# The row of 1/rms of the first feed-forward stage is turned inside the tail gate chunk

## The chip, the cores and the metric

The kernel runs on one core of a Trainium2 chip. The metric is device time in microseconds (us), the median of several runs. Besides these runs one execution was recorded by the hardware profiler; every time that is read from a trace below belongs to that one execution. PE is TensorE (its weight loads are listed apart as PEld), DVE is VectorE, ACT is ScalarE, POOL is GpSimd, and SP issues most of the DMAs.

## What is computed

One layer of an encoder: a half-step feed-forward stage (FFN), a mixing stage of Fourier and attention heads, a second FFN, and a last norm, on 512 tokens of width 1024, all in float32. The change lies in the opening of the first FFN:

```python
def rms_norm(x, g):
    xf = x.astype(jnp.float32)
    y = xf * lax.rsqrt(jnp.mean(xf * xf, axis=-1, keepdims=True) + EPS)
    return (y * g.astype(jnp.float32)).astype(x.dtype)

def swiglu(h, w_gate, w_up, w_down):
    return (jax.nn.silu(h @ w_gate) * (h @ w_up)) @ w_down

x = x + 0.5 * swiglu(rms_norm(x, ffn1_norm), ffn1_w_gate, ffn1_w_up, ffn1_w_down)
```

## The kernel before

The activations lie transposed, features on partitions and tokens along the free dimension, as 8 tiles of 128x512 (`x[k]`). A float32 product is made of three passes of a fast format: every operand is split into a high part (a cast on ACT) and a low part (the rest, a subtraction on DVE: `lows`, L130, or, for some weights, a negation on ACT, L159, with a DMA from POOL that adds the original, L160), and high x high, high x low and low x high are summed in one PSUM bank.

The factor 1/rms of a token multiplies a whole row of the product, so it is put off: PE multiplies the gained but not yet normalised `x`, and the factor comes in when a bank is read. For that the factor has to lie along the free dimension, the same on all partitions. `Norm.sum` (L244) adds the squares with PE, `mean` (L251, DVE) and `power` (L258, POOL) give `r`, one factor per token in a column of 128x4, and `row` (L263, L271) turns it: four transposes on PE write the bank `rp`, and ACT copies that bank to `rb` in SBUF.

What reads `rp` and `rb` is the rest of the opening:

- `evacuate` (L659 to L674) reads the gate and up banks of one chunk pair with `rb` (DVE), takes the silu (ACT), multiplies (DVE) and splits the product into its high and low parts `at` (L663 ACT, L130 DVE). This also frees the banks for later chunks.
- `operands` (L349 to L356 and L359) makes, for i = 0 to 3, the tile `b_i` from `x`, the gains and `rp`, then the differences `t_i`, and splits them into the parts `rt`. These are what the later groups of the stage multiply, by a Strassen-like scheme of seven products (`seven`). The tile `b_i` lies in a pool of two buffers, which it shares with `raw_g`, the gate weights of that scheme; so the load of the first `raw_g` waits until everything that reads `b_2` is done.

PE and SP follow the order in which the program is written. On ACT and DVE that holds for the first half of the opening; after it the order of their instructions is worked out when the program is built, by a scheduler that has its own costs. Every engine then runs its instructions in that order.

PE's order in the opening is: the products of chunks 0 to 3 over k = 0 to 7 (L769, twelve matmuls for each k), the tail chunk 42 (`gate(2 * NF)`, 24 matmuls, the 64 last gate and 64 last up columns), the chunks 4 to 7 (24 matmuls each), and then the down projections dn_0 to dn_7 of this group of chunks (11 matmuls each). The weights of dn_d are loaded by SP (`raw_dn`), cast by ACT (L172) and given their low part by DVE (L130); the third matmul of dn_d is the first to read that low part. SP's queue has, after `raw_dn` 0 to 2, the first `raw_g` and `raw_u`, and behind them `raw_dn` 3 to 7.

The row is turned at (k, n) = (7, 4), that is, after the first four of the twelve matmuls of k = 7. The second FFN gives its own place for it (`gate(1, {3: row})`).

Of the kernel before, what the change touches and what calls it, by code (L numbers as in the profile page):

```python
# [18 lines left out]
NF = F // P  # L19
# [69 lines left out]
def encoder(ctx, tc, A, out):  # L89
# [19 lines left out]
    def bank(name):  # L109
        return pp.tile([P, S], F32, tag="bank", name=name)  # L110
# [68 lines left out]
    def turned(ap):  # L179
        return ap.rearrange("p (a b c) -> p b a c", b=4, c=4)  # L180
# [12 lines left out]
    class Norm:  # L193
# [71 lines left out]
        def row(self, c0=0, c1=4):  # L265

            ps = bank(f"rp{self.n}_{c0}")
            for c in range(c0, c1):
                self.turn(ps, c)
            t = slice(c0 * P, c1 * P)  # L270
            nc.scalar.copy(self.rb[:, t], ps[:, t])  # L271
            return ps
# [11 lines left out]
    def ffn(norm, after, wgu, wd, wdt, groups, opening, closing):  # L284
# [6 lines left out]
        with tc.tile_pool(name=f"act{n_}", bufs=1) as ap, tc.tile_pool(name=f"sums{n_}", bufs=2) as sp:  # L291
# [7 lines left out]
            def place(j):  # L299
                where[j] = free.pop(0)  # L300
                return where[j]
# [8 lines left out]
            def gate(c, between={}, by_dma=False):  # L310
                whi, wlo = weights(wgu[c], f"gu{n_}_{c}", by_dma=by_dma)
                ps = bank(f"gu{n_}_{c}")
                for k in range(KD):
                    between.get(k, int)()
                    product(ps, whi[:, k, :], wlo[:, k, :], hh[k], hl[k], k == 0, k == KD - 1, turn=True)
                return ps
# [48 lines left out]
            def back(ts):  # L365
                plain[:] = [t for t in plain if all(t is not q for q in ts)]
# [213 lines left out]
            for gi, group in enumerate(groups):  # L580
                last = gi == len(groups) - 1
                ahead = []
                if gi:
                    rest = seven(range(group[0] + 1, min(group[-1] + 2, NF)), ready)
                else:
                    lent = [acts[:, FRONT + i * KD * P : FRONT + (i + 1) * KD * P] for i in range(PLACES - 4, PLACES)]
                    plain.extend(lent)
                    row = []
                    pss = dict(enumerate(opening(gate, lambda: norm.column([norm.acc]), lambda: row.append(norm.row()))))
                    back(lent[:2])  # L590
                    due, parts, left = [*pss, "t"], list(range(KH)), range(2 * len(pss), 2 * n_plain)
                    pss["t"] = [gate(2 * NF)]
                    tail_weights()
                    for i, c in enumerate(left):
                        pss.setdefault(c // 2, []).append(gate(c, by_dma=i in (1,) if n_ else i > 0))
                        if due:
                            j = due.pop(0)
                            evacuate(at[:, place(j)], n_, pss[j], norm)
                        if c % 2 and c != left[-1]:
                            due.append(c // 2)  # L600
                        while len(parts) * len(left) > (len(left) - 1 - i) * KH:
                            o = parts.pop(0)
                            operands(row[0], o, o + 1)

                    def rest():
                        evacuate(at[:, place(n_plain - 1)], n_, pss[n_plain - 1], norm)
# [114 lines left out]
    def opening1(gate, column, row):  # L721

        pss = [bank(f"gu0_{c}") for c in range(4)]
        ws = []
        ts = slice(0, HALF), slice(HALF, S)
        cs = slice(0, 2), slice(2, 4)

        def highs(i, k):
            n0.scale_high(k)
            hi, _ = ws[i]  # L730
            nc.scalar.copy(hi[:, k % 2], raws[i][:, k % 2])

        def first_operands():

            hi, lo = ws[0]
            for t, c in zip(ts, cs):
                n0.scale_high(0, nc.vector, t)
                n0.scale_low(0, t)
                nc.scalar.copy(hi[:, 0, c], raws[0][:, 0, c])
            for c in cs:  # L740
                lows(lo[:, 0, c], raws[0][:, 0, c], hi[:, 0, c])

        def first_products():

            hi, lo = ws[0]
            for t, c0, m in [(ts[0], c, m) for c in cs for m in (hh, hl)] + [(ts[1], c, m) for m in (hh, hl) for c in cs]:
                for c in range(c0.start, c0.stop):
                    nc.tensor.matmul(
                        turned(pss[c][:, t]), hi[:, 0, c], turned(m[0][:, t]), start=m is hh and t is ts[0], stop=False,
                        skip_group_check=True,  # L750
                    )
            for c in range(4):
                nc.tensor.matmul(
                    turned(pss[c]), lo[:, 0, c], turned(hh[0]), start=False, stop=False, skip_group_check=True
                )

        def weight_lows(i, k):
            hi, lo = ws[i]
            lows(lo[:, k % 2], raws[i][:, k % 2], hi[:, k % 2])

        def products(k):
            hi, lo = ws[k // 2]
            passes = [(c, w, m) for w, m in ((hi, hh), (hi, hl), (lo, hh)) for c in range(4)]
            for n, (c, w, m) in enumerate(passes):
                if (k, n) == (6, 8):
                    sums()
                if (k, n) == (7, 4):
                    row()
                nc.tensor.matmul(  # L769
                    turned(pss[c]), w[:, k % 2, c], turned(m[k]), start=False, stop=k == KD - 1 and w is lo,  # L770
                    skip_group_check=True,
                )

        ss = []

        def sums():
            ss.append(bank("ss0"))
            for c in range(4):
                n0.sum(ss[0], c, [n0.acc])

        with tc.manual_schedule(engines={mybir.EngineType.Activation, mybir.EngineType.DVE}):
            for k in range(KD):
                i = k // 2
                if k % 2 == 0:
                    ws.append(tuple(slot().rearrange("p (a c b) -> p a c b", a=2, b=P) for _ in range(2)))
                if k == 0:
                    first_operands()
                    continue
                highs(i, k)
                if k < KD - 1:  # L790
                    n0.scale_low(k)
                    weight_lows(i, k)
                for j in {3: range(0, 4), 5: (4, 5), 6: (6, 7)}.get(k, ()):
                    n0.sums(j)
            first_products()
            for k in range(1, KD - 1):
                products(k)
            n0.scale_low(KD - 1)
            n0.mean(ss[0], 0, 4)
            n0.power(0, 4)  # L800
            weight_lows(KH - 1, KD - 1)
            products(KD - 1)
        nc.sync.dma_start(out=qkg, in_=A["qkg"])
        nc.sync.dma_start(out=fb, in_=A["fb"])
        return [pss[0:2], pss[2:4]]
# [795 lines left out]
```

## Time and profile before

| what | value |
|---|---|
| median of 3 runs | 818.72 us |
| lowest and highest run | 818.27 and 1692.98 us |
| time of the profiled execution | 818.38 us |
| its span, first to last instruction | 816.6 us |
| busy: PE, DVE, ACT, POOL | 99%, 80%, 62%, 8% of the span |
| granted TensorE clock, mean | 0.998 |

The median and the profiled execution agree within 0.34 us; one of the three runs took twice as long. Between span and time of the profiled execution lie 1.8 us. In a row of the timeline stand the start and the duration in us, the engine, the line, the operation, what it writes and reads, its shape, how many instructions are merged in the row, and in brackets the idle time of the engine before it with what ended it. Rows of one engine overlap a little: the next instruction starts some 0.08 us before the end of the last on DVE, some 0.1 us on ACT, and a matmul every 0.22 us though one is listed with 0.38 us.

### The profile page before, as it was taken

How to read it: one execution, taken by the hardware profiler on the slowest of the kernel's cores; microseconds unless marked ns; L12 is line 12 of the kernel's file. 1: busy time of each engine (PE TensorE's matmuls, PEld its weight loads, DVE VectorE, ACT ScalarE, POOL GpSimd, SP SyncE). 2: the span in 40 equal slices, each digit the busy share in tenths (PEclk: the TensorE clock that was granted, in tenths of full speed). 3: DMA queues.
4: the chain of work that ended last, by engine and by line, in shares of the span. 5: the costliest groups of instructions: out<-in, count | busy, mean ns of one | idle time of the engine just before them, and what ended most of it. 6: DMA issues, size and time to landing. Idle time of an engine off the chain costs nothing.

```text
span 816.6 us, 13031 instructions
## 1 busy us (share of the span) xinstructions
PE 809.8 (99%) x4943; PEld 729.3 (89%) x4943; DVE 652.4 (80%) x1083; ACT 503.2 (62%) x871; POOL 67.7 (8%) x75
## 2 busy tenths in 40 slices
PE   9999999999999999999999999999999999999997
PEld 7888998899989998889998888889988998899987
DVE  7997997489856857799998578999955997489674
ACT  7873774267624735699998449557733674267462
POOL 0320000000000000221000003100100000000001
PEclk9999999999999999999999999999999999999999
DMA  7874553345443423442201236554543553345222
GB/s 258 198 172 172 146 132 89 125 130 168 85 151 89 126 67 117 130 149 65 65 26 53 78 109 140 128 188 143 133 116 110 154 145 81 132 130 143 62 78 103
DMA packets 37823, 99.75 MB, mean 122 GB/s; under 512 B 4481, under 2 KB 11265, under 8 KB 37761
## 3 DMA queue, kind: packets, MB, share of 16 engines
q1 hardware_dynamic: 28064, 82.87, 31.2%
q0 software_dynamic: 8832, 15.34, 11.1%
q8 instruction: 38, 0.62, 0.3%
q10 hardware_dynamic: 864, 0.72, 0.3%
q14 instruction: 25, 0.20, 0.1%
HBM read 93.41 MB, written 2.10 MB: 117 GB/s over the span
## 4 chain that ended last, share of the span: by engine, by line
PE 94%; DMA 2%; ACT 1%; DVE 1%; issue 1%; POOL 0%; SPq 0%; POOLq 0%; DVEq 0%; ACTq 0%
PE dn L186 26%; PE r L436 11%; PE mix L186 8%; PE gu L186 8%; PE r L441 8%; PE q L436 4%; PE r L432 4%; PE q L441 4%; PE p L432 4%; PE q L432 4%; PE p L441 2%; PE mix L1267 2%; PE mix L1233 2%; PE mix L1071 1%; PE mix L1072 1%; PE mix L1073 1%
## 5 line engine op out<-in xcount | busy, mean ns | idle before, releaser
L186 PE MATMUL dn<-at,ring 128*128 128x512 f32 x900 | 202.7, 380 | 0.0
L186 PEld LDWEIGHTS dn<-at,ring 128*128 128x128 f32 x900 | 168.0, 188 | 28.9 <-DVE ring L130 0.3
L441 PE MATMUL r<-rt,ring 128*128 128x256 f32 x560 | 154.3, 276 | 0.0
L436 PE MATMUL r<-rt,ring 128*128 128x256 f32 x840 | 147.0, 276 | 0.0
L436 PEld LDWEIGHTS r<-rt,ring 128*128 128x128 f32 x840 | 127.0, 188 | 1.6
L441 PEld LDWEIGHTS r<-rt,ring 128*128 128x128 f32 x560 | 105.1, 188 | 0.2
L391 ACT CAST ring<-s 128x1024 fp32r<-128x1024 f32 x70 | 73.6, 1051 | 35.4 <-PE r L436 16.4
L130 DVE TENSOR_TENSOR ring<-s,ring 128x1024 fp32r<-128x1024 f32 x70 | 85.1, 1216 | 12.6 <-ACT ring L391 10.3
L575 DVE SCALAR_TENSOR_TENSOR gx<-dn,gx 128x512 f32<-128x512 f32 x61 | 41.8, 688 | 63.0 <-PE dn L186 63.0
L172 ACT CAST ring<-raw_dn 128x768 fp32r<-128x768 f32 (+3 forms) x58 | 45.3, 784 | 71.3 <-PE dn L186 55.2
L441 PE MATMUL q<-rt,ring 128*128 128x256 f32 x280 | 77.0, 275 | 0.0
L160 POOL DMA_DIRECT2D ring<-in_wgu x38 | 32.9, 866 | 470.1 <-ACT u L450 372.0
L130 DVE TENSOR_TENSOR ring<-raw_dn,ring 128x768 fp32r<-128x768 f32 (+3 forms) x58 | 51.5, 890 | 9.9 <-ACT ring L172 5.9
L441 PEld LDWEIGHTS q<-rt,ring 128*128 128x128 f32 x280 | 52.6, 188 | 0.0
L130 DVE TENSOR_TENSOR ring<-raw_g,ring 128x1024 fp32r<-128x1024 f32 x35 | 42.6, 1218 | 10.1 <-PE p L432 9.5
L436 PE MATMUL q<-rt,ring 128*128 128x256 f32 x280 | 49.8, 277 | 0.0
L432 PE MATMUL r<-rt,ring 128*128 128x512 f32 x140 | 48.7, 384 | 0.2 <-ACT u L489 0.2
L186 PE MATMUL gu<-ring 128*128 128x512 f32 x216 | 48.9, 381 | 0.0
L432 PE MATMUL q<-rt,ring 128*128 128x512 f32 x140 | 48.3, 382 | 0.0
L432 PE MATMUL p<-rt,ring 128*128 128x512 f32 x140 | 48.3, 382 | 0.0
L186 PEld LDWEIGHTS gu<-ring 128*128 128x128 f32 x216 | 40.4, 188 | 6.9
L391 ACT CAST ring<-raw_g 128x1024 fp32r<-128x1024 f32 x35 | 36.8, 1051 | 15.0 <-DMA raw_g<-in_wgu 12.0
(282 smaller groups left out, 1659.3 us busy)
## 6 DMA issues: line engine op xcount, KB each, us to landing
raw_g<-in_wgu SPq DMA_DIRECT2D x35, 512.0 KB, 3.7
raw_u<-in_wgu SPq DMA_DIRECT2D x35, 512.0 KB, 4.4
raw_dn<-in_wd SPq DMA_DIRECT2D x40, 384.0 KB, 3.2
ring<-in_wgu POOLq DMA_DIRECT2D x35, 256.0 KB, 4.3
raw_gu<-in_wgu SPq DMA_DIRECT2D x12, 512.0 KB, 3.6
raw_o<-in_wo SPq DMA_DIRECT2D x8, 512.0 KB, 3.5
raw_dn<-in_wd SPq DMA_DIRECT2D x8, 448.0 KB, 3.4
raw_wq<-in_wins SPq DMA_DIRECT2D x4, 512.0 KB, 3.6
```

The source lines that it names most:

```text
L130: nc.vector.tensor_tensor(out=lo, in0=src, in1=asf(hi), op=ALU.subtract)
L160: nc.gpsimd.dma_start(out=lo, in_=src, accum_op=ALU.add)
L172: nc.scalar.copy(hi[:, :n, :], raw[:, :n, :])
L186: nc.tensor.matmul(ps, a, b, start=first and b is mhi and a is whi, stop=last and a is wlo)
L391: nc.scalar.copy(hi, src)
L432: nc.tensor.matmul(turned(ps), whi[:, ks], turned(m), start=start, stop=False, skip_group_check=True)
L436: nc.tensor.matmul(ps[:, t], whi[:, ks], m[:, o * HALF :][:, t], start=start and o == 0, stop=False, skip_group_check=True,)
L441: nc.tensor.matmul(o, wlo[:, ks], m, start=False, stop=stop, skip_group_check=True)
L575: nc.vector.scalar_tensor_tensor(out=x[d][:, t], in0=ps[:, t], scalar=0.5, in1=x[d][:, t], op0=ALU.mult, op1=ALU.add)
L1071: nc.tensor.matmul(ps, hh[k][:, cs], whi[:, a, :], start=k == 0, stop=False)
L1233: nc.tensor.transpose(pts[n][:, c * P : (c + 1) * P], prob[t, b, c][:, kc * P : (kc + 1) * P], ident)
L1267: nc.tensor.matmul(turned(outs[t, b]), w, turned(p), start=kc == 0 and i == 0, stop=kc == 3 and i == 1)
```

## The change

The row is no longer turned within the products of chunks 0 to 3, but one chunk later, within the tail chunk, before its products of k = 1, that is, after its first three matmuls. The second FFN, whose opening has filled `row` by then, is built as before.

```diff
-                    pss["t"] = [gate(2 * NF)]
+                    pss["t"] = [gate(2 * NF, {} if row else {1: lambda: row.append(norm.row())})]
...
                 if (k, n) == (6, 8):
                     sums()
-                if (k, n) == (7, 4):
-                    row()
                 nc.tensor.matmul(
```

On PE and SP nothing else moves, and on POOL one DMA of the opening goes ahead of two others; lines behind the removed ones have a number lower by two. ACT and DVE get another order in the whole opening. In the rows below, `gu_c` is the bank and `raw_gu_c` the raw weights of chunk c, `g0p` and `u0p` are the gate and up tiles of an evacuation, `s_0_4` are sums of weights of the first `raw_g` and `raw_u`, and `dn_d` is the bank of a down projection.

ACT, around the copy of the row (L271), before:

```order
L172 CAST ring<-raw_gu_4_354 128x1024
L271 COPY rb_102<-rp_0_298 128x512
L172 CAST at_129<-raw_gu_5_408 128x1024
L359 CAST rt_130<-b_0_391 128x256
L159 ACTIVATE at_129<-at_129 128x1024
L359 CAST rt_130<-b_0_391 128x2x256
```

ACT, the same place, now:

```order
L172 CAST ring<-raw_gu_4_354 128x1024
L172 CAST at_129<-raw_gu_5_408 128x1024
L159 ACTIVATE at_129<-at_129 128x1024
L271 COPY rb_102<-rp_0_317 128x512
L661 ACTIVATE g0p<-g0p 128x512
L359 CAST rt_130<-b_0_391 128x256
```

The copy of the row now stands behind the cast and the negation of the weights of chunk 5.

DVE, from the last subtraction that reads `b_2` (its third row `t_2_506`) to the low part of the weights of dn_2, before:

```order
L356 TENSOR_TENSOR t_2_506<-b_2_503,t_2_506 128x256
L130 TENSOR_TENSOR rt_130<-t_2_506,rt_130 128x3x256
L356 TENSOR_TENSOR t_3_562<-b_3_559,t_3_562 128x256
L130 TENSOR_TENSOR at_129<-u0p,at_129 64x512
L659 TENSOR_TENSOR g0p<-gu_6_469,rb_102 128x512
L130 TENSOR_TENSOR rt_130<-t_3_562,rt_130 128x3x256
L130 TENSOR_TENSOR at_129<-u0p,at_129 128x512
L130 TENSOR_TENSOR rt_130<-t_2_506,rt_130 128x256
L130 TENSOR_TENSOR rt_130<-t_3_562,rt_130 128x256
L130 TENSOR_TENSOR ring<-raw_dn_2_0_620,ring 128x384
```

DVE, up to that same subtraction, which is the last row here, now:

```order
L356 TENSOR_TENSOR t_3_562<-b_3_559 128x256 x2
L130 TENSOR_TENSOR at_129<-u0p,at_129 64x512
L662 TENSOR_TENSOR u0p<-g0p,u0p 128x512
L659 TENSOR_TENSOR g0p<-gu_6_469,rb_102 128x512
L356 TENSOR_TENSOR t_2_506<-b_2_503,t_2_506 128x256
L356 TENSOR_TENSOR t_3_562<-b_3_559,t_3_562 128x256
L130 TENSOR_TENSOR ring<-raw_dn_2_0_620,ring 128x384
L130 TENSOR_TENSOR at_129<-u0p,at_129 128x512
L356 TENSOR_TENSOR t_2_506<-b_2_503,t_2_506 128x256
```

Four instructions that stood behind that subtraction stand ahead of it now: the low parts of `u0p` (64x512 and 128x512), the reading of bank gu_6, and the low part of the weights of dn_2.

DVE, from the low part of the first `raw_g` on, with the low part of the weights of dn_3 (`raw_dn_3`), before:

```order
L130 TENSOR_TENSOR ring<-raw_g_4_635,ring 128x1024
L406 TENSOR_TENSOR s_0_4_639<-raw_u_4_636 128x512
L406 TENSOR_TENSOR s_0_4_640<-raw_g_4_635,raw_u_4_636 128x512
L660 TENSOR_TENSOR u0p<-gu_7_526,rb_102 128x512
L406 TENSOR_TENSOR s_0_4_639<-s_0_4_639,raw_g_4_635 128x512
L575 SCALAR_TENSOR_TENSOR gx<-dn_0_0_577,gx 128x512
L130 TENSOR_TENSOR at_129<-raw_dn_3_0_645,at_129 128x384
L662 TENSOR_TENSOR u0p<-g0p,u0p 128x512
L406 TENSOR_TENSOR s_0_4_640<-raw_g_4_635,s_0_4_639 128x512
L575 SCALAR_TENSOR_TENSOR gx<-dn_1_0_602,gx 128x512
```

DVE, the same place, now:

```order
L660 TENSOR_TENSOR u0p<-gu_7_526,rb_102 128x512
L130 TENSOR_TENSOR rt_130<-t_3_562,rt_130 128x3x256
L130 TENSOR_TENSOR rt_130<-t_2_506,rt_130 128x256
L130 TENSOR_TENSOR rt_130<-t_3_562,rt_130 128x256
L662 TENSOR_TENSOR u0p<-g0p,u0p 128x512
L575 SCALAR_TENSOR_TENSOR gx<-dn_0_0_577,gx 128x512
L130 TENSOR_TENSOR ring<-raw_g_4_635,ring 128x1024
L406 TENSOR_TENSOR s_0_4_639<-raw_u_4_636 128x512
L406 TENSOR_TENSOR s_0_4_640<-raw_g_4_635,raw_u_4_636 128x512
L575 SCALAR_TENSOR_TENSOR gx<-dn_1_0_602,gx 128x512
L130 TENSOR_TENSOR at_129<-u0p,at_129 128x512
L130 TENSOR_TENSOR at_129<-raw_dn_3_0_645,at_129 128x384
```

Ahead of the low part of `raw_dn_3` now stand L662, L575 of dn_1 and one more low part of `u0p`, which stood behind it; one L406 that stood ahead of it stands behind it.

## The prediction

> **What bounds the kernel now.** I read the page first, then PE's waits over the whole run, then the timeline of the opening engine by engine. The first fence is the page's row of busy times, then PE's waits (us in total, times, longest).
>
> ```profile
> PE 809.8 (99%) x4943; PEld 729.3 (89%) x4943; DVE 652.4 (80%) x1083; ACT 503.2 (62%) x871; POOL 67.7 (8%) x75
> ...
> PE busy L702 <- PEq L1584: 0.8, 1, 0.8
> PE rp L263 <- POOL r L258: 0.6, 1, 0.6
> PE r L432 <- ACT u L489: 0.2, 1, 0.2
> ```
>
> PE is the bound nearly everywhere, so a change counts by what it does to PE's few waits. The second wait, 0.6 us, is the row being turned before POOL has made `r`. The timeline shows it:
>
> ```profile
> 22.88 2.04 PE L769 MATMUL gu<-ring,at 128*128 128x512 f32 x8
> 23.94 1.53 POOL L258 TENSOR_TENSOR r<-ms,mhalf 128x4 f32<-128x4 f32 x1 [22.63 <-DVE ms L251]
> 25.52 0.65 PE L263 MATMUL rp<-ident,r 128*128 128x128 f32 x4 [0.60 <-POOL r L258]
> 25.93 2.01 PE L769 MATMUL gu<-ring,at 128*128 128x512 f32 x8
> 27.78 10.72 PE L186 MATMUL gu<-ring 128*128 128x512 f32 x48
> ```
>
> One matmul is issued every (10.72 - 0.38)/47 = 0.22 us. The last one ahead of the transposes starts at 22.88 + 2.04 - 0.38 = 24.54, so the next could start at 24.76; the transposes start at 25.52. The loss is 0.76 us of issue time, a little more than the listed 0.60.
>
> The second thing to see is DVE. The windows view gives, for the stretch from DVE's first use of the row to its first later idle time, length, then busy time and count of PE, PEld, DVE, ACT and POOL, PEclk, DMA share and GB/s:
>
> ```profile
> 26.83:54.45 27.62, 27.62 (x128) 23.55 (x127) 27.50 (x52) 24.94 (x44) 10.13 (x10) 1.00 0.91 203
> ```
>
> DVE works 27.50 of 27.62 us: its queue is full for 28 us, and it begins when the row is there. PE is not held only because everything it takes from that queue comes just early enough.
>
> **The change part by part.** *PE's wait goes.* `r` is ready at 23.94 + 1.53 = 25.47. After the change eight matmuls (1.76) and three of the tail chunk (0.66) go from 24.76 on, so PE comes to the transposes at 27.18, 1.7 us after `r`. The four transposes are the same four; their price moves with them. Gain: 0.76 us. The cover is good, since the 1.7 us do not hang on any other transfer.
>
> *The row comes later to ACT.* `rp` is complete at 27.18 + 0.65 = 27.83 instead of 26.17. But by the new order its copy (L271) stands behind the cast and the negation of the weights of chunk 5. These are their rows, the copy's, and the load of those weights with its time to landing:
>
> ```profile
> 26.21 0.59 ACT L271 COPY rb<-rp 128x512 f32<-128x512 f32 x1 [1.42 <-PE rp L263]
> 27.36 1.05 ACT L172 CAST at<-raw_gu 128x1024 fp32r<-128x1024 f32 x1 [0.56 <-PE gu L769]
> 28.62 1.06 ACT L159 ACTIVATE at<-at 128x1024 fp32r<-128x1024 f32 x1
> 29.58 0.60 ACT L359 CAST rt<-b 128x512 fp32r<-128x512 f32 x1
> ...
> 23.74 0.33 SPq L154 DMA_DIRECT2D raw_gu<-in_wgu  x1
> ...
> DMA to landing us min/median/max: 3.5/3.5/3.5
> ```
>
> The cast needs its weights, which land at 23.74 + 3.5 = 27.24, hardly before the matmul that the page names as its releaser. That matmul will be over sooner, the landing will not: the cast starts at about 27.3. The negation reads what the cast writes and starts at 27.3 + 1.05 = 28.35; the next instruction follows 0.96 later (28.62 to 29.58 above), so the copy starts at 29.3 and ends at 29.9. Who waits behind it: all of DVE's new order starts with L659, which reads `rb`.
>
> *DVE starts later.* Its rows that carry the rest:
>
> ```profile
> 26.83 2.72 DVE L349 SCALAR_TENSOR_TENSOR b<-gx,rp 128x512 f32<-128x512 f32 x4 [0.79 <-ACT rb L271]
> ...
> 48.78 0.42 DVE L356 TENSOR_TENSOR t<-b,t 128x256 f32<-128x256 f32 x1
> ...
> 50.43 0.69 DVE L130 TENSOR_TENSOR at<-u0p,at 64x512 fp32r<-64x512 f32 x1
> 51.16 0.69 DVE L659 TENSOR_TENSOR g0p<-gu,rb 128x512 f32<-128x512 f32 x1
> ...
> 52.63 0.68 DVE L130 TENSOR_TENSOR at<-u0p,at 128x512 fp32r<-128x512 f32 x1
> ...
> 53.90 0.55 DVE L130 TENSOR_TENSOR ring<-raw_dn,ring 128x384 fp32r<-128x384 f32 x1
> 54.81 1.22 DVE L130 TENSOR_TENSOR ring<-raw_g,ring 128x1024 fp32r<-128x1024 f32 x1 [0.35 <-ACT ring L391]
> 55.95 0.68 DVE L406 TENSOR_TENSOR s<-raw_u 128x512 f32<-128x512 f32 x1
> ...
> 58.95 0.55 DVE L130 TENSOR_TENSOR at<-raw_dn,at 128x384 fp32r<-128x384 f32 x1
> ```
>
> Start 29.95 instead of 26.83: 3.1 us late. A full queue can't make that up; it can only be reordered. The place where PE feels it is dn_3, whose low weights are the last row above (end 59.50). PE's row:
>
> ```profile
> 61.44 0.82 PE L186 MATMUL dn<-at 128*128 128x512 f32 x3
> ```
>
> The third of these matmuls, at 61.44 + 0.44 = 61.88, is the first that reads them: they are 2.4 us early. After the change: 59.50 + 3.1 for the later start; plus three instructions that now stand ahead (L662, L575 of dn_1, a low part of `u0p`) less one that now stands behind (L406), each about 0.60 to the next start, so + 1.2; less DVE's idle time before 54.81, which is filled (0.35 + 0.08 of overlap). That is 63.4.
>
> *A second way to the same place.* SP's first `raw_g` waits for the readers of `b_2`, and `raw_dn` 3 is queued behind it. SP's waits and the load's rows:
>
> ```profile
> SPq L383 <- DMA rt<-b: 10.4, 2, 7.9
> ...
> 50.27 0.33 SPq L383 DMA_DIRECT2D raw_g<-in_wgu  x1
> ...
> DMA to landing us min/median/max: 3.4/3.4/3.4
> ```
>
> Before, a DMA that reads `b_2` ended that wait; DVE's last subtraction had ended at 48.78 + 0.42 = 49.20. After, that subtraction ends 3.1 later and behind four more instructions (0.61 + 0.60 + 0.60 + 0.47 = 2.3, from the rows at 50.43 to 53.90, less the overlap): 54.6. The load is issued then and lands at 58.0; ACT's cast takes 1.05 (as the one of chunk 5, the same shape), so DVE can take the low part of `raw_g` at 59.1. It gets there by its own queue at about 59.2. The two ends fall together, so DVE does not idle and neither alone would save much. From 59.15: 1.14 to the next start, four instructions of 0.60, then 0.55: 63.2 to 63.3. I take 63.3.
>
> *The sum.* Without a new wait PE would want that low part at 61.88 - 0.76 = 61.12. It gets it at 63.3: a new wait of 2.2 us. Net + 1.45 us, or, simpler, the third matmul of dn_3 starts at 63.3 instead of 61.88, and the gain is lost within the wait. Behind it PE goes on at its old pace: the low part of dn_4 follows in DVE's queue directly, 0.47 later, and each dn takes PE 11 x 0.22 = 2.4 us. From the group behind, the orders are the same again. So 818.38 + 1.4 = 819.8 us. The profiled run stands 0.34 under the median of the runs shown, which I take into the range.
>
> Bounds: the term that no row shows is how the reordered DVE queue meets ACT's. Were DVE never kept waiting by ACT, 63.3 stands; were every one of the three instructions moved ahead of `raw_dn` 3 to find its input late by its own 0.60, it is 65.1, net + 3.2. From below, if the cast of chunk 5 did not hold up the copy (27.9 instead of 29.3), the wait shrinks by 1.4 to 0.8 and the net is nothing. I take the middle value since all its steps are rows.
>
> One moved DMA needs a price, that of POOL for chunk 6, which goes ahead of two of `b_1`. The negation ahead of it, the DMA with its landing, and PE's chunk 6:
>
> ```profile
> 34.17 1.06 ACT L159 ACTIVATE ring<-ring 128x1024 fp32r<-128x1024 f32 x1
> ...
> 35.53 0.91 POOL L160 DMA_DIRECT2D ring<-in_wgu  x1 [0.98 <-ACT ring L159]
> ...
> DMA to landing us min/median/max: 6.3/6.3/6.3
> 43.62 1.70 PE L186 MATMUL gu<-ring 128*128 128x512 f32 x7
> ```
>
> It landed at 41.9; the third matmul of chunk 6 (44.06) wants it, after the change at 43.3. In ACT's new order the negation follows DVE's fifth instruction, which ends at 29.95 + 2 x 0.60 + 2 x 0.66 + 0.68 = 33.15 (L659, L660, two L349, L659), and then a silu and a small cast (at most 0.59 each, as the copy) and a cast of 0.95 to the next start: 35.1 at most instead of 34.17. Landing 0.9 later, at 42.8, leaves 0.5 us. [...]
>
> **The rivals.** *Only the gain* (not slower): DVE makes up its late start and dn_3 finds its low part in time. Then 818.38 - 0.76 = 817.6. It decides if the low part ends before 61.1. For it speaks that PE now waits nowhere behind the opening; against it the 27.50 of 27.62 and the two chains that end together. Chance 0.12.
>
> *The clock falls.* A wait of 2.2 us is longer than any that PE has in this trace. At the end of the run and at its start the trace shows (windows view, then PE's rows):
>
> ```profile
> 813.40:816.60 3.20, 0.00 (x0) 0.00 (x0) 0.00 (x0) 0.00 (x0) 0.00 (x0) 0.50 0.50 165
> ...
> 810.64 0.74 PE L1428 MATMUL xt<-ident,gx 128*128 128x128 f32 x5
> 0.78 3.57 PE L702 MATMUL busy<-const-bfloat16-1.0 128*128 128x512 bf16 x8 [0.78 <-PEq L1584]
> ```
>
> PE's last work ends at 811.38, and from 813.4 on the granted clock is 0.50: two idle microseconds were enough there. At the start eight matmuls take 3.57 us, 0.45 each, double the 0.22 of later. If the new wait dropped the clock, PE would lose about as much as there, half of 3.6: 1.8 us, 821.6 in all. [...] Chance 0.12.
>
> *The wait comes at chunk 6 instead*, if POOL's DMA lands over 0.5 us later than I have it. PE then loses that time at 43 us, but has it back in a shorter wait at dn_3, which DVE sets: 819.8 again, and up to 820.8 if DVE's evacuations are held too. Chance 0.06.
>
> That the change does nothing is excluded by the orders.
>
> **How the numbers follow.** Forecast as summed, 0.70: 819.8, with its own range 818.8 to 821.0. The range of eight in ten leaves out most of the first rival and reaches to the clock case: 818.1 to 821.6. Two per cent, about what a measurement of this kernel can tell from no change, is 16.4 us; no case here comes near it, on either side. Faster 0.01, same 0.97, slower 0.02, the rest being what I have not thought of.
>
> **What would show it.** The changed profile has no wait of `rp` on POOL's `r`; ACT's copy of the row starts near 29.3 and DVE's first L659 near 29.95; the first `raw_g` is issued near 54.6, ended by DVE; PE has one new wait of about 2.2 us in a `dn` on DVE, near 61 to 63, with the clock at 1.00 after it; and from about 75 us on all is as before, shifted by 1.4. A new wait at another place, or none, would make the prediction wrong.

## The result, and the profile after

The changed kernel takes 823.54 us (median of six executions, 821.39 to 824.01) beside 818.58 us of the kernel before: ratio 1.0052, 95% interval 1.0037 to 1.0068. On two other chips, in the experiments below, it was 1.0040 (1.0027 to 1.0053) and 1.0047 (1.0034 to 1.0059). That is slower by half a per cent: over the forecast of 819.8 and over the range, whose end was 821.6.

The six times fall into two groups. Two stand at 821.4 and 821.5 with a mean granted clock of 0.999, four between 823.4 and 824.0 with 0.997. The profiled execution, 824.01 us with a span of 822.2, is one of the four. First PE's new waits (us in total, times, longest).

```profile
PE dn L186 <- DVE at L130: 2.5, 2, 2.0
PE dn L186 <- ACT at L172: 0.9, 1, 0.9
```

The wait for `r` is gone. In its place PE waits three times in the first `dn` group. The timeline of the same execution shows the way there, engine by engine; ahead of it the row of before that fixes the opening's time, the 32 matmuls which the loads of the opening release.

```profile
15.04 7.20 PE L769 MATMUL gu<-ring,at 128*128 128x512 f32 x32
```

```profile
15.80 7.20 PE L767 MATMUL gu<-ring,at 128*128 128x512 f32 x32
...
25.55 1.53 POOL L258 TENSOR_TENSOR r<-ms,mhalf 128x4 f32<-128x4 f32 x1 [24.24 <-DVE ms L251]
...
27.97 0.60 PE L263 MATMUL rp<-ident,r 128*128 128x128 f32 x4
...
28.91 1.05 ACT L172 CAST at<-raw_gu 128x1024 fp32r<-128x1024 f32 x1 [2.51 <-DMA raw_gu<-in_wgu]
29.99 1.06 ACT L159 ACTIVATE at<-at 128x1024 fp32r<-128x1024 f32 x1
30.95 0.57 ACT L271 COPY rb<-rp 128x512 f32<-128x512 f32 x1
...
31.55 0.69 DVE L659 TENSOR_TENSOR g0p<-gu,rb 128x512 f32<-128x512 f32 x1 [3.90 <-ACT rb L271]
...
55.27 1.06 PE L186 MATMUL dn<-at 128*128 128x512 f32 x4
56.85 0.72 PE L186 MATMUL dn<-at 128*128 128x512 f32 x2 [0.53 <-DVE at L130]
...
57.21 0.33 SPq L383 DMA_DIRECT2D raw_g<-in_wgu  x1
...
60.78 1.05 ACT L391 CAST ring<-raw_g 128x1024 fp32r<-128x1024 f32 x1 [2.87 <-DMA raw_g<-in_wgu]
...
60.94 1.50 PE L186 MATMUL dn<-at,ring 128*128 128x512 f32 x6
63.34 0.72 PE L186 MATMUL dn<-at 128*128 128x512 f32 x2 [0.90 <-ACT at L172]
...
65.41 0.55 DVE L130 TENSOR_TENSOR at<-raw_dn,at 128x384 fp32r<-128x384 f32 x1
...
66.01 0.61 PE L186 MATMUL dn<-at 128*128 128x512 f32 x1 [1.96 <-DVE at L130]
...
67.28 2.63 PE L186 MATMUL dn<-at 128*128 128x512 f32 x6
```

Four things are to be seen. The row is turned at 27.97 without a wait, 0.9 us after `r` is there (25.55 + 1.53), but its copy (L271) runs only at 30.95, behind the cast and the negation of chunk 5's weights, and that cast waited 2.51 us for its load. DVE, idle for 3.90 us, starts with the row at 31.55. DVE's low part of dn_3 ends at 65.96, and PE's first matmul that reads it starts at 66.01. And the six matmuls from 67.28 take 2.63 us instead of the 1.50 of the six at 60.94: they run at about half speed.

By issue times (a matmul every 0.22 us) the three waits cost 0.70 (56.85 less 55.27 + 4 x 0.22), 1.08 (63.34 less 60.94 + 6 x 0.22) and 2.23 us (66.01 less 63.34 + 2 x 0.22): 4.0 in all. The gain of 0.76 and the opening, 0.76 later in this execution (15.80 against 15.04), cancel. So the third matmul of dn_3 starts at 66.01 instead of 61.88, 4.1 us later; the spans differ by 5.6, and the other 1.5 us come with the half clock:

```profile
62.82:66.23 3.42, 0.94 (x3) 0.52 (x4) 3.42 (x7) 1.41 (x4) 0.92 (x1) 1.00 0.19 57
66.23:69.65 3.41, 3.41 (x9) 2.67 (x9) 3.41 (x6) 1.46 (x2) 0.00 (x0) 0.50 0.98 195
69.65:73.06 3.41, 3.41 (x17) 2.90 (x17) 2.69 (x5) 1.78 (x3) 0.00 (x0) 1.00 0.89 343
```

These are rows of the windows view: stretch, length, busy time and count of PE, PEld, DVE, ACT and POOL, then the granted clock. For 3.41 us it is 0.50: nine matmuls instead of seventeen, 8 x 0.22 = 1.8 us. (0.3 us of it come back near 113 us, where PE in the profile of before has its wait of `r` on ACT at L432, and here none.)

### The profile page after: what moved, and what is told of

It reads as the page before. It is cut to its first block, busy times and chain, and to the rows that moved or that the text cites. A ratio compares the mean times of both kernels' runs of the same rounds, so it can differ in the third digit from the quotient of the medians.

```text
span 822.2 us, 13029 instructions
## 1 busy us (share of the span) xinstructions
PE 812.6 (99%) x4943; PEld 730.2 (89%) x4943; DVE 652.7 (79%) x1083; ACT 502.9 (61%) x871; POOL 67.5 (8%) x75
## 4 chain that ended last, share of the span: by engine, by line
PE 90%; ACT 3%; DMA 2%; DVE 2%; issue 1%; SPq 0%; POOL 0%; DVEq 0%; POOLq 0%; ACTq 0%
PE dn L186 25%; PE r L436 12%; PE mix L186 8%; PE r L441 8%; PE gu L186 5%; PE q L436 4%; PE q L441 4%; PE r L432 4%; PE q L432 4%; PE p L432 4%; PE p L441 2%; PE mix L1265 2%; PE mix L1231 2%; PE mix L1070 1%; PE mix L1069 1%; PE mix L1071 1%
## 5 line engine op out<-in xcount | busy, mean ns | idle before, releaser
L575 DVE SCALAR_TENSOR_TENSOR gx<-dn,gx 128x512 f32<-128x512 f32 x61 | 41.8, 688 | 63.4 <-PE dn L186 63.2
L432 PE MATMUL r<-rt,ring 128*128 128x512 f32 x140 | 48.8, 385 | 0.0
L432 PE MATMUL q<-rt,ring 128*128 128x512 f32 x140 | 48.3, 382 | 0.0
L432 PE MATMUL p<-rt,ring 128*128 128x512 f32 x140 | 48.3, 382 | 0.0
```

The costliest lines, as they stand in the source:

```text
L432: nc.tensor.matmul(turned(ps), whi[:, ks], turned(m), start=start, stop=False, skip_group_check=True)
L575: nc.vector.scalar_tensor_tensor(out=x[d][:, t], in0=ps[:, t], scalar=0.5, in1=x[d][:, t], op0=ALU.mult, op1=ALU.add)
```

## The experiments

Two theories of the cost went in, and their rivals. *Queues:* the copy of the row, behind chunk 5's cast and negation in ACT's queue, starts DVE late, and DVE's full queue brings dn_3's low weights late. *Clock:* that wait drops the clock in some executions. The rivals: the opening's loads came late in the changed program, and that is the cost; the place of the transposes on PE is the cost, not ACT's queue; the clock falls by itself. Times are medians; "before" is the kernel before, measured beside it on the same chip.

**The changed kernel again**, twice, on two chips.

> The changed kernel once more, unaltered. Theory (queues): ACT copies the row behind the cast and the negation of chunk 5's weights, DVE starts late with a full queue, PE waits in dn_0 and dn_3, and a long enough wait there halves the granted clock for one stretch of 3.4 us (1.7 us lost). So: 821.3 to 821.6 in executions without the half clock, 823.4 to 824.0 in those with it, nothing between; PE's new waits together 2.2 to 3.4 us; the opening's loads, 1.1 us late in the first profile, land anywhere between there and where they landed before the change. Rival (loads): the changed program always gets its opening loads 1.1 us later, and that is where most of the time is: the last raw_first lands at 14.8 us again, not at 13.8. Rival (clock by itself): the half clock comes in executions whose waits in dn_3 are no longer than in the others, or at another place than right behind them.

> The changed kernel unaltered, as the measure for the run with the low part written twice, and a third profile of it. 819.5 to 822.1 in executions with the clock whole, 822.8 to 825 in those with a half clock, the latter about half of them. By the share of a window: in the profile every window of 3.41 us, counted from where the clock first rises, in which PE works under 0.45 is followed by one at half clock, and none with 0.5 or more is.

Measured: 822.06 us (nine executions, 819.57 to 825.02; before 819.10), and 823.89 us (six, 821.22 to 824.30; before 819.17). Over the three measurements of the changed kernel 12 of 21 executions have a mean clock of 0.997 or less, and these are exactly the ones at 822.8 us and above; of the 72 executions of the kernel before in this section none is under 0.998. The two groups are there, but wider than expected: 819.57 to 822.45 with the clock whole (median 821.4), 822.84 to 825.02 with less (median 823.8). The profile of the first repeat has the clock whole:

```profile
15.64 7.20 PE L767 MATMUL gu<-ring,at 128*128 128x512 f32 x32
...
27.91 1.05 ACT L172 CAST at<-raw_gu 128x1024 fp32r<-128x1024 f32 x1 [2.65 <-DMA raw_gu<-in_wgu]
...
29.95 0.57 ACT L271 COPY rb<-rp 128x512 f32<-128x512 f32 x1
...
30.55 0.69 DVE L659 TENSOR_TENSOR g0p<-gu,rb 128x512 f32<-128x512 f32 x1 [4.03 <-ACT rb L271]
...
45.09 1.41 DVE L349 SCALAR_TENSOR_TENSOR b<-gx,rp 128x512 f32<-128x512 f32 x2 [0.35 <-DMA rt<-b]
...
59.92 1.50 PE L186 MATMUL dn<-at,ring 128*128 128x512 f32 x6
61.98 0.72 PE L186 MATMUL dn<-at 128*128 128x512 f32 x2 [0.56 <-ACT at L172]
...
64.05 0.55 DVE L130 TENSOR_TENSOR at<-raw_dn,at 128x384 fp32r<-128x384 f32 x1
...
64.66 0.49 PE L186 MATMUL dn<-at 128*128 128x512 f32 x1 [1.96 <-DVE at L130]
```

Here the waits cost 0.74 (61.98 less 59.92 + 1.32) and 2.24 us, 2.98 together; less the gain of 0.76, plus the opening's 0.60 (15.64 against 15.04), that is 2.8, and the third matmul of dn_3 starts 2.78 us later than before. The span is 819.5, 2.9 above 816.6. So without the half clock the account closes to 0.1 us. The opening's lateness belongs to the execution, not to the change: in the profiles of this study that row lies between 14.95 and 15.93, and the one of before is an early one. In that form the loads rival falls; what stays of it comes below.

**The copy ahead of the cast.** PE's order as in the changed kernel; chunk 5's cast is put behind the copy in ACT's queue.

```
 # norm.row
-            nc.scalar.copy(self.rb[:, t], ps[:, t])
+            self.turned = nc.scalar.copy(self.rb[:, t], ps[:, t]).ins
 # weights, the cast of the high part
-            nc.scalar.copy(hi[:, :n, :], raw[:, :n, :])
+            with tc.issue_after(n0.turned) if name == "gu0_5" else nullcontext():
+                nc.scalar.copy(hi[:, :n, :], raw[:, :n, :])
```

> The changed kernel with PE's order as it is, but with the cast of chunk 5's weights put behind the copy of the row in ACT's queue. Theory (queues): the copy starts 0.1 to 0.2 us after the transposes are complete, near 28.0 instead of 29.4 (on the clock of an execution whose opening is not late), DVE starts 1.4 earlier, PE's wait in dn_3 shrinks to under 1.0 us, no half clock: 818.2 to 819.6. Rival (the place alone): that the row is turned 1.7 us later on PE is the cost, and the ACT queue costs nothing: waits as before within 0.5 us, 820.8 to 823.5.

Measured: 819.55 us, ratio to before 1.0010 (1.0001 to 1.0018); the changed kernel on the same chip 822.06.

```profile
27.73 0.59 ACT L271 COPY rb<-rp 128x512 f32<-128x512 f32 x1 [3.11 <-PE rp L263]
28.22 1.05 ACT L172 CAST at<-raw_gu 128x1024 fp32r<-128x1024 f32 x1
...
28.35 0.69 DVE L659 TENSOR_TENSOR g0p<-gu,rb 128x512 f32<-128x512 f32 x1 [2.47 <-ACT rb L271]
...
62.80 0.49 PE L186 MATMUL dn<-at 128*128 128x512 f32 x1 [1.62 <-DVE at L130]
```

With the transposes where the change put them, 2.5 us come back when the copy no longer stands behind the cast; between the executions with the clock whole it is 1.9 (medians 819.5 and 821.4). The time is as the theory had it, but two things are not. One of the eleven executions, 822.63 us, has a clock of 0.996, where none was expected. And the wait, 1.62 us, is longer than the 1.0 I allowed. The windows row of DVE's path, from its first use of the row to the end of dn_3's low part, says why:

```profile
28.35:62.75 34.40, 32.82 (x150) 27.64 (x148) 33.41 (x62) 27.73 (x49) 10.93 (x11) 1.00 0.73 154
```

DVE starts earlier, but it still needs 34.40 us, where the kernel before needs 32.67: the order that came with the change puts more work ahead of dn_3's low part, and that is not the copy's doing.

**The row within the last step**, behind the seventh matmul instead of the fourth, and, one matmul further, behind the eighth. Against the kernel before:

```
-                if (k, n) == (7, 4):
+                if (k, n) == (7, 7):        # and (7, 8)
                     row()
```

> The kernel before, with the row turned three matmuls later within the products of the last step (behind the seventh of twelve instead of behind the fourth), not a chunk later. Theory (queues): three matmuls (0.66 us) go where PE waited 0.76 for r, the transposes run at 25.5 as before, the copy still comes ahead of chunk 5's cast, and DVE starts as before: 0.5 to 0.76 us under the kernel before, 817.6 to 818.1. Rival: the gain at the transposes is never worth anything, since DVE's queue sets the time behind it: 818.3 to 818.8 with a new wait of 0.6 us in a dn.

> The row behind the seventh of twelve matmuls of the opening's last step, once more, beside the next run. ACT copies the row ahead of chunk 5's cast. 0.5 to 0.9 us under the kernel before, as in the first run.

> The row behind the eighth of the twelve matmuls instead of behind the seventh: on PE 0.22 us later, but in ACT's order this flips the copy of the row behind the cast of chunk 5's weights, which waits for their load. Theory (queues): the copy starts when that cast is nearly over, 1.2 to 2.5 us later than with the seventh, DVE as well, and PE waits 0.5 to 1.5 us for low weights in a dn; 0.4 to 1.6 us above the run with the seventh. Rival (the place alone): the same within 0.3 us.

Measured: with the seventh 818.25 us beside 819.10 (0.9990, 0.9982 to 0.9999), and on another chip 818.36 beside 819.17 (0.9989, 0.9980 to 0.9997); with the eighth, on that chip, 818.94 (0.9998, 0.9989 to 1.0006). The first gain, 0.85 us, is a little over the 0.76 expected at most. The two kernels differ by one matmul on PE, but in ACT's order the copy and the cast change places, and DVE's order changes with them. ACT with the seventh, and ACT and PE with the eighth:

```profile
26.68 0.59 ACT L271 COPY rb<-rp 128x512 f32<-128x512 f32 x1 [1.42 <-PE rp L263]
27.72 1.05 ACT L172 CAST at<-raw_gu 128x1024 fp32r<-128x1024 f32 x1 [0.45 <-DMA raw_gu<-in_wgu]
```

```profile
28.20 1.05 ACT L172 CAST at<-raw_gu 128x1024 fp32r<-128x1024 f32 x1 [2.52 <-DMA raw_gu<-in_wgu]
29.15 0.58 ACT L271 COPY rb<-rp 128x512 f32<-128x512 f32 x1
...
62.45 0.49 PE L186 MATMUL dn<-at 128*128 128x512 f32 x1 [0.29 <-DVE at L130]
```

In the first the copy waits for the transposes, in the second the whole queue waits 2.52 us for a load that the row has nothing to do with. Counted from the opening's row of 32 matmuls (15.12 and 15.91), the copy starts 1.68 us later, as expected. The wait of 0.29 us is shorter than the 0.5 to 1.5 expected. The price is 0.6 us between the medians, at the low end of what I gave; the executions overlap (817.55 to 819.18, and 818.23 to 819.83), so the rows carry the theory better than the times. DVE's path has the same length in both, 32.60 and 32.64 us, so here the other order of DVE costs nothing. The version with the seventh matmul is faster than the kernel before, by 0.8 us.

**The row earlier or later in the tail chunk.** `{1: ...}` becomes `{0: ...}`, then `{2: ...}`.

> The changed kernel with the row turned one step (three matmuls, 0.66 us) earlier, ahead of the tail chunk's first matmul; ACT copies it between the cast and the negation of chunk 5's weights instead of behind both. Theory (queues): the copy starts about 1.06 us earlier, DVE with it, and PE's waits in the dn go down by about as much or more, to 0 to 1.5 us; half clock rare; 818.0 to 820.0. Rival (the place alone): 0.66 us earlier on PE is worth at most 0.66: 820.8 to 823.

> The changed kernel with the row turned one step (three matmuls, 0.66 us) later within the tail chunk. Theory (queues): the transposes end 0.66 us later, but ACT is at chunk 5's negation until then or later anyway, so the copy starts at most 0.2 us later and the time stays within 0.6 us of the changed kernel, half clock in about half of the executions. Rival (the place alone): 0.66 us or more are added.

Measured, both on one chip (before 818.86): 819.59 us, 1.0008 (1.0000 to 1.0017), with one wait of 0.79 us in dn_3; and 821.92 us, 1.0038 (1.0023 to 1.0053), with waits of 0.50 and 1.95, three of its six executions at 820.0 to 820.8 and three at 823.0 to 823.9. The changed kernel was not run on that chip; against the kernel before it stood 3.0 to 5.0 us higher on the others. One step earlier leaves 0.7 of that, one step later adds nothing: the cost does not go by PE's place. It is not all the copy, though. DVE's path in the earlier version:

```profile
30.37:62.82 32.45, 31.72 (x145) 26.70 (x143) 32.19 (x60) 26.79 (x48) 10.94 (x11) 1.00 0.74 153
```

It is 32.45 us, in the changed kernel 34.05 to 34.41. Counted from the row of 32 matmuls (15.86 here, 15.64 in the second profile), DVE starts only 0.4 us earlier than there, 14.51 instead of 14.91. So most of what this version wins over the changed kernel comes with DVE's order, and the copy has the smaller share.

**dn_3's load earlier.** SP issues `raw_dn` 3 ahead of the first `raw_g`; ACT's cast and DVE's low part follow it forward.

```
-                    while len(downs) < min(d + 1 + (0 if gi or not n_ else 2), KD):
+                    while len(downs) < min(d + 1 + (0 if gi else 2 if n_ else d == 2), KD):
```

> The changed kernel with one load moved: SP issues raw_dn 3 ahead of the first raw_g and raw_u instead of behind them, and with it ACT's cast and DVE's low part of dn_3 come some instructions earlier; PE's order and the late copy of the row stay as they are. Theory (queues: it is the place of dn_3's weights behind the wait for b_2 that turns the late start into a wait): the copy still starts late, behind chunk 5's negation, and DVE still starts about 3 us later than before the change, but PE has no wait over 0.5 us in dn_3, the clock stays, and the gain at the transposes remains: 0.4 to 0.8 us under the kernel before. Rival (a full DVE queue loses what it starts late, wherever it is): the wait moves to dn_4 to dn_7 or to the group behind, 2 to 3 us in all, and the time stays within 0.7 us of the changed kernel.

Measured: 819.86 us beside 818.86, 1.0009 (1.0001 to 1.0018). PE's waits:

```profile
PE dn L186 <- DVE ring L130: 0.8, 1, 0.8
...
65.11 0.49 PE L186 MATMUL dn<-at,ring 128*128 128x512 f32 x1 [0.77 <-DVE ring L130]
```

Neither expectation holds. No wait is left in dn_3, and 1.0 us above before is about a third or less of what the change cost elsewhere, so the place of dn_3's weights in the queues did carry most of it. But the wait moves on to dn_4, whose low weights were next in line, and takes the gain: what DVE starts late is partly lost wherever it is put. The profiled execution is the fastest of the eleven, 818.90 us, so 0.77 need not be all that the others lose.

**Matmuls of zeros where PE waits.** Four ahead of dn_3's first matmul, eight ahead of the first that reads the low weights; they add nothing to the sum.

```
-            product(ps[:, t], whi[:, k, :], wlo[:, k, :], h, l, first, last, cut, turn)
+            (hold if first and (n_, gi, d) == (0, 0, 3) else product)(ps[:, t], whi[:, k, :], ...)
+    def hold(ps, whi, wlo, h, l, *rest):
+        for n, (a, b) in enumerate([(z, one[1])] * 4 + [(whi, turned(h)), (whi, turned(l))]
+                                   + [(z, one[1])] * 8 + [(wlo, turned(h))]):
+            nc.tensor.matmul(ps if a is z else turned(ps), a, b, start=n == 0, stop=False)
 # first version: z in a new tile of 4 bytes a partition; second: in `table`, which nobody reads
```

> The changed kernel with 12 more matmuls of zeros that add nothing to dn_3: 4 ahead of its first matmul and 8 ahead of the first one that reads its low weights, 0.22 us each, 2.6 us in all, where PE waited 0.90 and 1.96. Theory (queues, then clock): PE works where it waited, the low weights still come when DVE makes them, so no half clock in any execution and 821.2 to 821.8 in all of them. Rival (clock by itself): still 823.4 to 824.0 in about four of six. Rival (no wait there worth filling): 2.6 us are added, 824 to 826.

> As the run with the 12 matmuls of zeros, but the zeros stand in a tile that the kernel had already (one whose content nobody reads), so no tile of the kernel moves to another address. Theory (queues, then clock): no half clock in any execution, 0.6 to 1.6 us under the changed kernel's median with no execution above 822.5; and the 21 us of the earlier run came from the moved addresses, so every matmul is back to 0.22 us. Rival (clock by itself): about half of the executions at 822.8 or above, clock 0.997, as for the changed kernel. Rival (the bf16 matmuls themselves cost the 21 us): 842 to 844 again.

Measured: 843.10 us in the first version, 822.47 in the second (821.24 to 823.11; before 818.86). In the second, the mean clock of all five executions is 0.998 or 0.999, and PE has no wait in a `dn`. The time missed what I expected by about a microsecond, and two executions are above 822.5. The profiled one, 822.82 us, has a wait late in the program that the changed kernel does not have:

```profile
754.89 0.94 ACT L172 CAST ring<-raw_dn 128x896 fp32r<-128x896 f32 x1 [3.29 <-DMA raw_dn<-in_wd]
...
757.62 0.49 PE L432 MATMUL r<-rt,ring 128*128 128x512 f32 x1 [1.50 <-ACT u L489]
```

The order of the instructions is the changed kernel's there. It is one load of weights that took 4.9 us to land, in the changed kernel's first profile 3.4; ACT's cast waits 3.29 us for it instead of 1.80, and its copy for PE stands behind that cast. Less these 1.5 us the execution would be at 821.3. Whether the other four have the same wait is not recorded, so the missing microsecond is explained for one execution only. The half clock is gone here, where PE is kept at work; five executions at 0.998 or 0.999, against 12 of 21 at 0.997 or less, support that, and the next run and the windows carry it. (Of the four executions of the first version one shows 0.997; its windows are not on record.)

**dn_3's low part written twice.** One more instruction of DVE. The edit is written out here as an `if`. I expected six other instructions between the two writings; in the trace there are three (they start at 64.76 and 66.90).

```
                 whi, wlo = weights(src, "", len(js), raw, skip=SKIP if halves_ else 0)
+                if (n_, gi, d) == (0, 0, 3):
+                    lows(wlo[:, :len(js)], raw[:, :len(js)], whi[:, :len(js)])
```

> The changed kernel with DVE's low part of dn_3 written twice; by the new order six other instructions of DVE stand between the two, so PE gets it 2.1 us later: one unbroken wait of 4.0 to 4.2 us in dn_3 instead of 1.96. [...] Share of a window: the clock is set by fixed windows of 3.41 us, and one in which PE works under about 0.45 of the time halves it for the next; with a wait this long such a window is there in every execution, so the half clock comes in all of them, 1.2 to 2.4 us on top of the 2.1: 824.0 to 826.5, all. [...]

Measured: 826.05 us (825.39 to 826.55; the changed kernel on the same chip 823.89), the clock between 0.995 and 0.997 in all four executions; PE's longest wait is 4.1 us, as expected. The windows, first of this kernel, then of the changed kernel's third profile, its second, and the end of the kernel before:

```profile
62.28:65.69 3.41, 0.72 (x2) 0.30 (x2) 3.41 (x7) 1.29 (x3) 0.92 (x1) 1.00 0.23 60
65.69:69.10 3.41, 1.60 (x4) 1.33 (x5) 3.41 (x7) 2.01 (x3) 0.00 (x0) 0.50 0.82 171
69.10:72.52 3.42, 3.42 (x10) 2.68 (x9) 2.44 (x3) 1.16 (x2) 0.00 (x0) 0.50 0.89 303
```

```profile
60.74:64.15 3.41, 1.55 (x6) 0.67 (x4) 3.38 (x5) 2.40 (x6) 0.72 (x1) 1.00 0.12 45
64.15:67.56 3.41, 2.64 (x6) 2.15 (x7) 3.41 (x8) 1.47 (x2) 0.20 (x1) 0.50 0.84 155
67.56:70.98 3.42, 3.42 (x9) 2.64 (x8) 2.67 (x5) 1.46 (x2) 0.00 (x0) 0.50 1.01 350
```

```profile
60.41:63.82 3.41, 1.73 (x7) 0.82 (x5) 3.33 (x6) 2.46 (x6) 0.65 (x1) 1.00 0.20 74
63.82:67.24 3.42, 2.58 (x12) 2.20 (x13) 3.42 (x7) 1.46 (x2) 0.26 (x1) 1.00 0.83 167
```

```profile
809.95:813.36 3.41, 1.44 (x12) 1.20 (x10) 2.31 (x6) 1.38 (x4) 0.55 (x1) 1.00 1.02 356
```

The stretches are not chosen freely. In the first profile and in the one of before, the clock's record changes only at whole multiples of 3.413 us after its start: in the first, which starts at 4.80 us, at 66.23, 69.65 and 820.58 (18, 19 and 239 of them), in the other, from 4.41, at 813.37 (237). The stretches of the other profiles are counted in the same way, and the clock in each row above is 1.00 or 0.50. Read so, a window in which PE works 0.94, 0.72, 1.55 or 1.44 us of its 3.41 is followed by one at 0.50; one with 1.73, the first of the second profile, is not (the row behind it has 1.00), nor is one with 2.89 (55.99 to 59.41 in the first profile) or 2.81 (24.89 to 28.30 in the one of before). In none of the four that were followed by 0.50 was PE idle throughout. Behind a window with 1.60 (here) or 2.64 us (third profile) of work at half clock stands a second one at 0.50; behind a window worked throughout at half clock the row has 1.00 again (from 69.65 in the first profile, from 70.98 in the third).

## Why the prediction was wrong

**PE's wait for `r`, and its worth.** Right. The transposes run without a wait, and where the gain is bought without the late copy it is whole: 0.85 and 0.81 us of median difference with the seventh matmul, against 0.76. The cover was less firm than I said. In the first profile it was 0.9 us instead of 1.7, since `r` does hang on a transfer: DVE takes the mean behind the low parts of `wt`, and these wait for ACT's cast of `rawt`, which waited 1.44 us for its load there and 0.90 before.

**The copy behind chunk 5's cast and negation.** Right in mechanism; shown by the copy put ahead of them (1.9 us back with the clock whole) and by the rows of the seventh and eighth matmul. I took the landing of chunk 5's weights, 27.24, from the one profile of before, where nothing hung on it. Counted from the row of 32 matmuls I had the copy at 14.26 us; the three profiles of the changed kernel have 15.15, 14.31 and 14.12, and the cast's rows say why: it waits 2.4 to 2.7 us for that load, and starts when the load pleases. This is what stays of the loads rival.

**DVE's path to dn_3.** Here the sum was mis-sized, in its term "less DVE's idle time before 54.81, which is filled (0.35 + 0.08 of overlap)". The windows from DVE's first use of the row to the end of dn_3's low part, before, in the changed kernel's first profile and in its second (the third busy time is DVE's):

```profile
26.83:59.50 32.67, 32.67 (x151) 27.86 (x150) 32.19 (x60) 28.06 (x49) 11.04 (x11) 1.00 0.83 184
```

```profile
31.55:65.96 34.41, 31.08 (x139) 25.52 (x137) 33.48 (x62) 25.68 (x47) 10.73 (x11) 1.00 0.72 146
```

```profile
30.55:64.60 34.05, 31.59 (x143) 26.28 (x141) 33.49 (x62) 25.68 (x47) 10.74 (x11) 1.00 0.71 146
```

The instructions that moved ahead add 33.49 - 32.19 = 1.3 us of work, near the 1.2 predicted. But the idle time was not filled: 0.48 before, 0.56 and 0.93 after, since the new order meets a wait of its own (0.35 us for the transfer out of `b`, before 45.09). The path took 34.05 us and more instead of 33.35, and that 0.7 is nearly the whole difference in the second profile: 2.98 us lost by issue times instead of 2.2. The second way to the same place came as described, only later: the first `raw_g` was issued at 57.21 in the first profile instead of 54.6, 1.85 of it beyond the later opening, and at 55.95 in the second, 0.75 beyond it. Both ways do end nearly together, as I had it: DVE waits for ACT's cast of `raw_g` 0.19 us in the first profile. In the first, the late load and more idle time made it 4.0.

**The new wait.** I had one wait of 2.2 us. It was two, the first on ACT's cast of dn_3's high weights, and in one profile of three a third in dn_0, on a low part of `u0p` that ends at 56.80. They go back to one cause, DVE's late and longer queue: its low parts come late, and by way of the first `raw_g` so does the cast, which stands in ACT's queue behind that of `raw_g` (at 60.78 in the first profile, after 2.87 us of waiting for that load). That POOL's transfer for chunk 6 would still be in time was right, no profile has a wait there. In the first profile luck helped: it was issued at 37.92 instead of 35.53 and landed in 5.7 us, at 43.6, ahead of 44.05 (43.61 + 0.44), when PE wanted it; with the 6.3 us that I took it would have been 0.2 late. As forecast, the orders are the same again from the group behind, and nothing more is lost there (2.78 us at dn_3, 2.9 at the end of the second profile).

**The clock.** The step that failed: together with the longer path it took the result out of the range. "The clock falls" had a chance of 0.12, with 1.8 us; it came in 12 of 21 executions and costs 1.5 us in the first profile (one window) and 2.9 in the third (two: a span of 822.5, 5.9 above before, less the 3.0 by which dn_3 starts later). Without it, 821.4 would have been the time, inside the range though not near 819.8; and with it alone, at my price, 821.6, the end of the range. No run shows a ground for so low a chance; what the runs show is that 0.94 and even 1.55 us of work in a window of 3.413 us did not hold the clock. The profile of before had the answer: the last window in which PE works, 809.95 to 813.36, holds 1.44 us of work and was followed by half clock. I had quoted that end and measured from the last matmul instead of by windows. The second and the third profile have nearly the same waits (0.56 and 1.96 us, 0.67 and 1.96), but 1.73 us of work in the window there, and 1.55 here, and only here the clock fell. How much of such a wait comes to lie in one window depends on where the windows stand, and their grid starts at 4.80 us in the first profile and at 4.41 in the one of before; I take it that this is why the same kernel has two groups of times.

**Order or late start.** No edit moved the copy and left DVE's order alone, but the paths side by side tell the two apart. With the seventh and the eighth matmul and with the row first in the tail, DVE starts 12.18, 13.85 and 14.51 us after the row of 32 matmuls, and its path is 32.60, 32.64 and 32.45 us, that of the kernel before (11.79, 32.67). With the copy ahead of the cast it starts at 13.40, earlier than two of these, and needs 34.40, as the changed kernel does (14.72 to 15.75, and 34.05 to 34.41); with the row later in the tail it is 15.44 and 33.67. So it is not the late start that makes the path longer, but the order. In the second profile the start comes 3.1 us later than before, beyond the opening, and the path is 1.4 longer; 2.4 of the two together was slack that dn_3's low weights had.

**Open.** Why a load lands later in one execution than in another is not shown. And since no version has the changed kernel's late start with the old order, the split between start and order is read from the paths and not from times.

## What to carry over

When an instruction is moved, look at what stands ahead of it in the queue of the engine that uses its result: one matmul more on PE put a copy behind a cast that waited 2.52 us for a load. Look as well at what a new order puts ahead of the instruction that matters: here DVE's order cost nearly half as much as its late start. A load's landing on which nothing hung is no constant once something hangs on it; take its spread from several profiles (the cast of chunk 5 waited 2.39 to 2.65 us for one in the three of the changed kernel). And price a wait by the windows of the clock as well as by its length: here two microseconds of waiting cost one and a half to three more.

## What the hardware showed besides

What the profiles show of the clock: in the first and in the one of before it changed on a grid of 3.413 us. In four profiles a window in which PE worked 0.72 to 1.55 us (0.45 of it at most) was followed by one at 0.50, and in the second profile one with 1.73 us (0.51) by one at 1.00. At half clock a window with 2.64 us of work (0.77, third profile) was followed by a second one at 0.50, and one worked throughout by 1.00 (first and third).

The first version with zeros took 843.10 us, 21 more than the second, with the same matmuls, on another chip. It differs in one tile of 4 bytes a partition, and DVE, ACT and POOL run the same instructions in the same order but for the place of one memset. That the added tile moves the tiles allocated behind it, and that their addresses are the cause, is an estimate of mine; no run shows either. The largest group of matmuls, of the kernel before and of that version, by the view that groups them (count, busy us, mean ns):

```profile
L186 PE MATMUL dn<-at,ring 128*128 128x512 f32 x900 | 202.7, 380 | 0.0
```

```profile
L186 PE MATMUL dn<-at,ring 128*128 128x512 f32 x900 | 211.6, 392 | 0.1
```

With the zeros in a tile that was there already the group took 203.1 us. Whether one of the tiles does it was not tried.
